# AdaLN scale and shift of the first 256 features: products summed on VectorE instead of row sums on TensorE

## The chip, the cores and the metric

The kernel runs on one core of one Trainium2 chip. The metric is the device time of one execution in microseconds (us); the engines are TensorE (PE, with PEld for its weight loads), VectorE (DVE), ScalarE (ACT), GpSimd (POOL) and SyncE (SP), which issues the transfers.

## The reference

A two-layer trunk over 512 tokens of 1024 features: stick-breaking attention and a gated token-mixing MLP, each followed by a SwiGLU layer. Every sub-layer has an RMSNorm in front whose result is scaled and shifted by numbers that depend on a conditioning vector `c`:

```python
def ada_modulation(c, w, b):
    m = jax.nn.silu(c) @ w + b
    shift, scale, gate = jnp.split(m, 3, axis=-1)
    return shift[:, None, :], scale[:, None, :], gate[:, None, :]
...
shift, scale, gate = ada_modulation(c, mix_ada_w[i], mix_ada_b[i])
h = rms_norm(x, mix_pre_g[i]) * (1.0 + scale) + shift
...
y = stick_breaking_mixer(h, sb_w_qkv[j], sb_w_o[j])
```

This case is about scale and shift of the very first sub-layer, so about the first 66 us of the kernel.

## The kernel before

All matrices are multiplied in float32 by splitting each operand into a high part (fp32r) and a remainder: ScalarE writes the high part (`wh`, `hTh`), VectorE subtracts it from the source to make the remainder (`wl`, `hTl`), and TensorE does three matmuls high x high, high x low, low x high (`mm3`). Line 94 records every matmul, line 102 every transpose, line 70 nearly every VectorE operation, line 161 and 162 the splits of a weight, line 117 other splits, line 111 every load on SyncE.

**The head.** Four tiles of 128 tokens (`x`) are loaded. `norm0` squares one on ScalarE, takes root and reciprocal, and scales it on VectorE; `turn0` transposes it on TensorE in two groups of four blocks (`tp`), and ScalarE or VectorE copies the blocks to `xhT`, which holds features on the partitions. From then on the 1024 features go in eight blocks of 128 (k = 0 to 7). For block k, `h0` has ScalarE multiply by the scale and add the shift (`xhT`, line 701), and splits the result to `hTh` and `hTl`. Then TensorE takes it as the contraction block k of the first half of the values (`v_step`: four token tiles, 12 matmuls `v`) and of the first head pair's queries and keys (`qk0_step`: 6 matmuls `pq` and `pk`). So each block brings 18 matmuls, and can start only when its scale and shift are there.

**Scale and shift.** They are products of `sc` (silu of c, 8 columns of 128) with a 1024x256 piece of weights per block, on their way for two blocks at a time. For blocks 2 to 7, three pairs, `ada0_sum` has POOL clear an accumulator (`acc`, 128x512) and VectorE add eight weight pieces, each times its column of `sc`; then `sums0` sums over the partitions with four small matmuls against a column of ones (into `ab`, which `cols0` has started with the bias), and VectorE multiplies by the norm's gain. Blocks 0 and 1 are done apart: `row0` has TensorE multiply the pieces (128x256) by the columns of `sc` directly, accumulates a row of 256 in `ab`, VectorE copies the row, and two small matmuls turn its halves into columns; `scales` adds the bias and multiplies by the gain.

**The gate.** Its weights (`rawada`) are added on VectorE in the same way into `G` (128x1024), in the background (`bg0.step`), from block 6 on.

A scheduler sets the order of the instructions of each engine from the order in which the code is written; an engine works strictly in its order. Buffers: `acc` has two (`acch`, `accl`), the `ada` pieces eight, `ab` takes turns in two PSUM banks.

## Time and profile before

| | |
|---|---|
| runs | 1131.42, 1133.75, 1135.18 us; median 1133.75 |
| profiled execution | 1135.34 us; its span 1133.6 us, mean granted clock 0.996 |
| busy | PE 1110.1, PEld 997.3, DVE 940.2, ACT 596.7, POOL 29.6 us |
| transfers | 176.39 MB in 51357 packets, mean 156 GB/s |
| chain that ended last | PE 78%, DMA 8%, DVE 8%, ACT 3%, issue 2% |

The span is from the first to the last recorded instruction. In a timeline row the first number is the start in us from the span's start, the second how long the merged instructions took, then engine, line, operation, output<-input, shapes and count; in brackets stands the idle time before it and what ended it. A group's row has after the bar the busy us and the mean ns of one.

### The profile page before, as it was taken

Reading aid. Unit: us, or ns where it says so; the run is one execution under the profiler, and the core shown is the slowest. Engines: PE = TensorE matmul, PEld = TensorE weight load, DVE = VectorE, ACT = ScalarE, POOL = GpSimd, SP = SyncE. Lnnn points to the kernel's source line nnn. Section 1 sums busy time; section 2 is a strip of 40 time slices with the busy share of each in tenths; the row PEclk is TensorE's granted clock in tenths of the full one; section 3 lists DMA queues with packets and bytes.
Section 4 is the critical chain, followed back from the end, with each engine's and each line's share of the span. In section 5 each row is a group of like instructions: output and inputs, shape, how many; then the busy total and the mean of one; then the engine's idle time right before and its main releaser. Section 6 shows DMA issues by size and latency. Waiting matters only on the chain.

```text
span 1133.6 us, 18637 instructions
## 1 busy us (share of the span) xinstructions
PE 1110.1 (98%) x7404; PEld 997.3 (88%) x7404; DVE 940.2 (83%) x1248; ACT 596.7 (53%) x982; POOL 29.6 (3%) x53
## 2 busy tenths in 40 slices
PE   6999999999999999999999999999999999999997
PEld 4787787788999999998878889988999999999996
DVE  4988999967989889778686967769979898889996
ACT  5454665656655555563143626437455555565752
POOL 0020100000000000010000000001000000000000
PEclk9999999999999999999999999999999999999999
DMA  7966434224434344438887375234243444223242
GB/s 301 353 219 213 147 104 131 76 72 150 149 121 140 127 154 130 131 115 307 268 276 241 131 241 177 83 131 158 86 131 114 165 131 141 71 87 98 91 164 95
DMA packets 51357, 176.39 MB, mean 156 GB/s; under 512 B 6075, under 2 KB 9147, under 8 KB 51269
## 3 DMA queue, kind: packets, MB, share of 16 engines
q1 hardware_dynamic: 48708, 166.81, 44.5%
q0 software_dynamic: 2560, 8.39, 2.1%
q8 instruction: 58, 0.95, 0.3%
q14 instruction: 31, 0.25, 0.1%
HBM read 164.69 MB, written 8.39 MB: 153 GB/s over the span
## 4 chain that ended last, share of the span: by engine, by line
PE 78%; DMA 8%; DVE 8%; ACT 3%; issue 2%; SPq 0%; POOL 0%; DVEq 0%; ACTq 0%
PE r L94 31%; PE y L94 9%; PE pqk L94 6%; PE v L94 5%; PE X L94 4%; PE u L94 4%; PE gu L94 4%; DMA rawada<-in_ada 4%; PE Y L94 3%; PE av L94 2%; PE z L94 2%; PE tw L102 1%; PE Z L94 1%; PE W L94 1%; PE tp L102 1%
## 5 line engine op out<-in xcount | busy, mean ns | idle before, releaser
L94 PE MATMUL r<-Sh,wl 128*128 128x256 f32 x608 | 169.9, 279 | 0.0
L94 PE MATMUL r<-Sh,wh 128*128 128x256 f32 x608 | 169.8, 279 | 0.0
L94 PE MATMUL r<-Sl,wh 128*128 128x256 f32 x608 | 169.7, 279 | 0.0
L161 ACT ACTIVATE wh<-raw 128x1024 fp32r<-128x1024 f32 x87 | 91.7, 1060 | 120.3 <-PE y L94 56.1
L94 PE MATMUL y<-wh,as 128*128 128x512 f32 x480 | 150.8, 391 | 0.4 <-DVE G L70 0.4
L117 ACT ACTIVATE wh<-f 128x1024 fp32r<-128x1024 f32 x87 | 92.4, 1062 | 90.0 <-PE r L94 66.6
L70 DVE TENSOR_TENSOR wl<-f,wh 128x1024 fp32r<-128x1024 f32 x87 | 106.4, 1223 | 39.0 <-ACT wh L117 38.9
L162 DVE TENSOR_TENSOR wl<-raw,wh 128x1024 fp32r<-128x1024 f32 x87 | 105.9, 1221 | 34.5 <-ACT wh L161 34.0
L94 PEld LDWEIGHTS r<-Sh,wl 128*128 128x128 f32 x608 | 114.1, 188 | 0.0
L94 PEld LDWEIGHTS r<-Sl,wh 128*128 128x128 f32 x608 | 114.1, 188 | 0.0
L94 PEld LDWEIGHTS r<-Sh,wh 128*128 128x128 f32 x608 | 113.9, 187 | 0.0
L94 PEld LDWEIGHTS y<-wh,as 128*128 128x128 f32 x480 | 90.0, 188 | 19.2 <-DVE G L70 0.8
L94 PE MATMUL y<-wl,as 128*128 128x512 f32 x240 | 93.7, 390 | 0.0
L94 PE MATMUL r<-hTh,wh 128*128 128x256 f32 x304 | 88.8, 293 | 0.5 <-DVE gu L70 0.4
L94 PE MATMUL r<-hTl,wh 128*128 128x256 f32 x304 | 84.8, 279 | 0.0
L94 PE MATMUL r<-hTh,wl 128*128 128x256 f32 x304 | 79.9, 279 | 0.0
L94 PEld LDWEIGHTS r<-hTh,wh 128*128 128x128 f32 x304 | 57.0, 187 | 5.8 <-DVE gu L70 2.1
L94 PE MATMUL r<-hTh,b 128*128 128x256 f32 x304 | 59.8, 279 | 0.0
L117 ACT ACTIVATE wh<-rawx 128x1024 fp32r<-128x1024 f32 x38 | 40.3, 1062 | 32.8 <-PE r L94 30.9
L94 PEld LDWEIGHTS r<-hTl,wh 128*128 128x128 f32 x304 | 57.1, 188 | 0.1
L94 PEld LDWEIGHTS r<-hTh,wl 128*128 128x128 f32 x304 | 55.0, 188 | 0.0
L94 PE MATMUL gu<-hTh,wh 128*128 128x256 f32 x192 | 53.8, 280 | 0.0
(272 smaller groups left out, 2955.0 us busy)
## 6 DMA issues: line engine op xcount, KB each, us to landing
rawada<-in_ada SPq DMA_DIRECT2D x80, 512.0 KB, 4.8
rawy<-in_wy SPq DMA_DIRECT2D x38, 512.0 KB, 3.5
rawx<-in_wx SPq DMA_DIRECT2D x38, 512.0 KB, 4.3
raw<-in_wdown SPq DMA_DIRECT2D x22, 512.0 KB, 4.5
raw<-in_wdn SPq DMA_DIRECT2D x22, 512.0 KB, 3.6
raw<-in_wqk SPq DMA_DIRECT2D x16, 512.0 KB, 4.6
ada<-in_ada0p SPq DMA_DIRECT2D x12, 512.0 KB, 7.9
raw<-in_wgu SPq DMA_DIRECT2D x12, 512.0 KB, 3.8
```

Of the source, the lines that this page charges most:

```text
L70: b = getattr(nc.vector, op)(*args, **kw)
L94: b = nc.tensor.matmul(o, l, r, start=start, stop=stop, skip_group_check=True)
L102: last_tp[0] = nc.tensor.transpose(o, i, ident)
L117: act.activation(hi, src, AF.Copy)
L161: act.activation(h[:], raw[:], AF.Copy)
L162: last_low[0] = nc.vector.tensor_tensor(l[:], raw[:], h[:].bitcast(F32), ALU.subtract)
```

## The change

`row0` is gone. In its place `pair0` uses `ada0_sum` on a width of 256: POOL clears 128x256 of an accumulator, VectorE adds eight pieces of 128x256, and two small matmuls sum over the partitions. `scales` is as before.

```diff
-    def row0(raws):
-
-        ps = bank("ab0", "p")
-        for q, raw in enumerate(raws):
-            for k in range(4):
-                mm(ps[0:1, :256], sc[:, q * 4 + k : q * 4 + k + 1], raw[:, k, :], q + k == 0, q * 4 + k == 7)
-        row = stp.tile([P, 256], F32, tag="row", bufs=2, name=nm("row"))
-        dve.tensor_copy(row[0:1, :], ps[0:1, :256])
+    def pair0(raws, tag):
+
+        acc = ada0_sum(raws, 256, 4, tag)
         ps = bank("ab0", "p")
         for i in range(2):
-            mm(ps[:, i : i + 1], row[0:1, i * P : (i + 1) * P], oneb[0:1, 0:1], True, True)
+            mm(ps[:, i : i + 1], acc[:, i * P : (i + 1) * P], onec, True, True)
         return ps
...
-    ab0 = row0(a0)
+    ab0 = pair0(a0, "acch")
...
-    ab1 = row0(a1)
+    ab1 = pair0(a1, "accl")
```

The places in the order on which the steps rest are two. On VectorE, before, between the scaling of the third x tile (`x_3`) and the remainder of the first scaled block (`hTl_133`); `ab` with `add` and `mul` is the scale and shift of block 0, `wl_251` the remainder of the first value weight:

```order
L70 TENSOR_SCALAR x_3_97<-x_3_97,r_183 128x1024
L70 COPY xhT_130<-tp_49_207 128x2x128
L70 COPY xhT_131<-tp_49_207 128x2x128
L70 RECIPROCAL r_219<-sd_217 128x1
L70 TENSOR_SCALAR x_4_99<-x_4_99,r_219 128x1024
L70 COPY row_195<-ab_45_186 1x256
L162 TENSOR_TENSOR wl_251<-raw_105,wh_250 128x1024
L70 TENSOR_TENSOR ab_262<-ab_47_197,add 128x2
L70 TENSOR_TENSOR ab_262<-ab_262,mul 128x2
```

And after, from the copies on to the first sum of block 1 (`acc_186` is the accumulator of block 0, `acc_267` that of block 1):

```order
L70 COPY xhT_130<-tp_48_206 128x2x128
L70 SCALAR_TENSOR_TENSOR acc_186<-ada_5_101,sc,acc_186 128x256
L70 COPY xhT_131<-tp_48_206 128x2x128
L70 SCALAR_TENSOR_TENSOR acc_186<-ada_5_101,sc,acc_186 128x256
L70 RECIPROCAL r_218<-sd_216 128x1
L70 SCALAR_TENSOR_TENSOR acc_186<-ada_5_101,sc,acc_186 128x256
L70 TENSOR_SCALAR x_4_99<-x_4_99,r_218 128x1024
L70 SCALAR_TENSOR_TENSOR acc_186<-ada_5_101,sc,acc_186 128x256
L70 SCALAR_TENSOR_TENSOR acc_186<-ada_6_103,sc,acc_186 128x256 x3
L162 TENSOR_TENSOR wl_250<-raw_105,wh_249 128x1024
L70 SCALAR_TENSOR_TENSOR acc_186<-ada_6_103,sc,acc_186 128x256
L70 SCALAR_TENSOR_TENSOR acc_267<-ada_8_107,sc,acc_267 128x256
```

The eight sums lie between the x tile's steps, and the weight's split stands ahead of the last of them.

On TensorE, before, from the transposes of the second x tile to the first value matmuls:

```order
L102 MATMUL tp_49_207<-identt,x_2_95 128x128 x4
L94 MATMUL ab_45_186<-ada_5_101,sc 1x256 x4
L94 MATMUL ab_45_186<-ada_6_103,sc 1x256 x4
L102 MATMUL tp_54_222<-identt,x_3_97 128x128 x4
L102 MATMUL tp_55_229<-identt,x_3_97 128x128
L94 MATMUL ab_47_197<-oneb,row_195 128x1 x2
L102 MATMUL tp_55_229<-identt,x_3_97 128x128 x3
L102 MATMUL tp_56_236<-identt,x_4_99 128x128 x4
L102 MATMUL tp_57_243<-identt,x_4_99 128x128 x4
L94 MATMUL ab_65_268<-ada_8_107,sc 1x256 x4
L94 MATMUL ab_65_268<-ada_9_109,sc 1x256 x4
L94 MATMUL v_70_286<-wh_250,hTh_132 128x512
```

And after, from the third x tile's transposes to the small matmuls of block 0:

```order
L102 MATMUL tp_53_221<-identt,x_3_97 128x128 x4
L102 MATMUL tp_54_228<-identt,x_3_97 128x128 x4
L102 MATMUL tp_55_235<-identt,x_4_99 128x128 x4
L102 MATMUL tp_56_242<-identt,x_4_99 128x128 x4
L94 MATMUL ab_46_196<-oneb,acc_186 128x1 x2
L94 MATMUL v_68_284<-wh_249,hTh_132 128x512
```

Nothing is left between the transposes, and the small matmuls of block 1 (`ab_65_277<-oneb,acc_267`) have moved from behind 8 value matmuls of block 0 to behind all 12 and two of `pq`.

Further down, VectorE has one sum of the next accumulator between the add and the multiply of block 1 in both programs, and SyncE has the first value weight of the second half ahead of five gate weights in both, the second one ahead of them in the changed order alone.

## The prediction

> **What bounds the kernel now.** I read the page first, then the busy time by stretch, then the timeline of the first 66 us, because the order of instructions differs there alone: on every engine the two programs list the same instructions in the same order again before the attention's second head pair.

> ```profile
> PE 1110.1 (98%) x7404; PEld 997.3 (88%) x7404; DVE 940.2 (83%) x1248; ACT 596.7 (53%) x982; POOL 29.6 (3%) x53
> 48.00:57.00 9.00, 9.00 (x44) 7.54 (x45) 8.76 (x13) 3.89 (x7) 0.00 (x0) 1.00 0.87 353
> 57.00:66.00 9.00, 9.00 (x42) 7.44 (x41) 8.86 (x9) 4.66 (x9) 5.03 (x11) 1.00 0.59 190
> 66.00:110.00 44.00, 43.83 (x213) 34.50 (x212) 35.52 (x39) 21.73 (x38) 4.16 (x8) 1.00 0.73 228
> 110.00:400.00 290.00, 287.40 (x1984) 253.61 (x1983) 252.65 (x324) 170.47 (x307) 7.22 (x12) 1.00 0.39 123
> ```

> After the stretch's bounds and its length stand the busy times of PE, PEld, DVE, ACT and POOL, then the granted clock, the DMA share and GB/s. From 48 us on TensorE has work all the time. So the question is when it reaches the steady part: what the head gains or loses there shifts the end by the same amount, since no later idle time takes it up. VectorE is nearly as full (8.76 of 9.00 and 8.86 of 9.00 us): this is where the change adds work.

> In the head TensorE stops in front of every new pair of features:

> ```profile
> 24.26 0.50 PE L94 MATMUL v<-wh,hTh 128*128 128x512 f32 x1
> 29.39 0.50 PE L94 MATMUL v<-wh,hTh 128*128 128x512 f32 x1 [0.33 <-ACT hTh L117]
> 36.65 0.80 PE L94 MATMUL v<-wh,hTh 128*128 128x512 f32 x1 [1.06 <-ACT hTh L117]
> 47.92 0.50 PE L94 MATMUL v<-wh,hTh 128*128 128x512 f32 x1 [0.40 <-ACT hTh L117]
> 57.15 0.39 PE L94 MATMUL v<-wh,hTh 128*128 128x512 f32 x1
> ```

> These are the starts of features 0, 1, 2, 4 and 6. I call them V0, V1, V2, V4 and V6; the change is worth what it moves V6.

> **What it removes.** Two times 16 pieces of row sum on TensorE, two copies of a row, and the small transposes of that row:

> ```profile
> 13.22 4.99 PE L94 MATMUL ab<-ada,sc 128*1 128x256 f32 x16
> 20.71 3.61 PE L94 MATMUL ab<-ada,sc 128*1 128x256 f32 x16
> 18.83 0.60 PE L94 MATMUL ab<-oneb,row 1*128 1x1 f32 x4
> L70 DVE COPY row<-ab 1x256 f32<-1x256 f32 x2 | 0.8, 408 | 3.3 <-PE ab L94 3.3
> ```

> The 8.6 us of row sums are on TensorE's path: the transposes of x's third and fourth tiles queue behind the first group, V0 behind the second. The small matmuls are replaced by as many over the full accumulator, which I take at the same 0.60 us.

> **What it adds.** Sixteen multiply-adds of 128x256 on VectorE. The trace has none of that width, but the same operation at 512 and at 1024:

> ```profile
> L70 DVE SCALAR_TENSOR_TENSOR acc<-ada,sc,acc 128x512 f32<-128x512 f32 x24 | 18.0, 750 | 0.6
> L70 DVE SCALAR_TENSOR_TENSOR G<-rawada,sc,G 128x1024 f32<-128x1024 f32 x3 | 3.8, 1282 | 0.0
> L70 DVE TENSOR_TENSOR hTl<-xhT,hTh 128x512 fp32r<-128x512 f32 x8 | 5.2, 686 | 3.1 <-ACT hTh L117 3.0
> L70 DVE COPY xhT<-tp 128x256 f32<-128x256 f32 x4 | 1.5, 418 | 0.3 <-PE tp L102 0.3
> 38.24 4.68 DVE L70 SCALAR_TENSOR_TENSOR acc<-ada,sc,acc 128x512 f32<-128x512 f32 x6
> ```

> 512 columns more cost 1282 - 750 = 532 ns, so 256 fewer cost 266 less: 484 ns. Six that depend on each other take 4.68 us, so one starts (4.68 - 0.75) / 5 = 0.79 us after the other, 0.04 more than its duration; I take 0.52 us in a chain and 0.40 where an independent instruction lies between. Bounds: 0.42 (a copy of that size) and 0.75 (the 512 form). Two groups of eight are about 8 us; less the two row copies, VectorE gets some 7 us more, in a stretch in which it has little idle time after 30 us.

> **The walk to V0.** The rows it hangs on:

> ```profile
> 13.32 0.76 DVE L70 COPY xhT<-tp 128x256 f32<-128x256 f32 x2 [0.30 <-PE tp L102]
> 14.19 0.75 DVE L70 TENSOR_SCALAR x<-x,r 128x1024 f32<-128x1024 f32 x1
> 18.58 1.20 DVE L162 TENSOR_TENSOR wl<-raw,wh 128x1024 fp32r<-128x1024 f32 x1
> 19.89 0.16 DVE L70 TENSOR_TENSOR ab<-ab,mul 128x2 f32<-128x2 f32 x1
> 21.55 0.85 ACT L701 ACTIVATE xhT<-xhT,ab 128x512 f32<-128x512 f32 x1
> 22.43 0.63 ACT L117 ACTIVATE hTh<-xhT 128x512 fp32r<-128x512 f32 x1
> ```

> Now the scale is ready at 20.05 but ScalarE, behind the late transposes, takes it up at 21.55; hTh is ready at 23.1, and TensorE is still in the second row sum until 24.25. In the changed order VectorE starts summing at 13.66. With the two copies, the reciprocal and the x tile between them, seven sums end near 18.0; the wl split comes ahead of the eighth (18.0 to 19.2), the eighth ends at 19.6. The x tile comes about 1.1 us later than now, which its transposes (done by 18) and ScalarE (done by 18.6) absorb. Two small matmuls to 20.25, add, one sum of the next group, multiply at 20.75 to 20.9; scale and split as now: V0 at 22.5, 1.75 us earlier. This is all the change gains.

> **From V0 to V1.** Between 18 and 22.5 TensorE now has only the small matmuls. What a gap does to its clock:

> ```profile
> 26.26:29.68 3.42, 3.09 (x17) 2.65 (x17) 2.67 (x6) 1.79 (x3) 0.00 (x0) 1.00 0.90 315
> 33.09:36.50 3.41, 2.50 (x16) 2.12 (x15) 3.24 (x5) 1.94 (x3) 1.42 (x2) 1.00 0.50 156
> 36.50:39.92 3.42, 3.27 (x8) 2.62 (x9) 3.35 (x6) 1.68 (x3) 0.00 (x0) 0.50 0.92 334
> 37.24 0.63 PE L94 MATMUL v<-wl,hTh 128*128 128x512 f32 x1
> 37.67 0.63 PE L94 MATMUL v<-wh,hTh 128*128 128x512 f32 x1
> 57.60 0.39 PE L94 MATMUL v<-wh,hTh 128*128 128x512 f32 x1
> 57.83 0.39 PE L94 MATMUL v<-wl,hTh 128*128 128x512 f32 x1
> ```

> After a stretch with 2.50 of 3.41 us busy the clock was 0.50 for 3.4 us, and matmuls started 0.43 us apart instead of 0.23; after one with 3.09 busy it stayed at 1.00. So V0's matmuls start at half clock, on the profile's own grid until 26.26: nine at 0.43, then five at 0.23, and the fourteen that stand ahead of the second small group end at 27.5 (bounds 25.7 at full clock throughout, 28.5 at half). VectorE has ended the second group at 25.4, with the hTl and wl splits in between, so TensorE, not VectorE, is last here.

> ```profile
> 26.30 0.60 PE L94 MATMUL ab<-oneb,row 1*128 1x1 f32 x4
> 26.93 0.16 DVE L70 TENSOR_TENSOR ab<-ab,add 128x2 f32<-128x2 f32 x1 [0.69 <-PE ab L94]
> 27.67 0.15 DVE L70 TENSOR_TENSOR ab<-ab,mul 128x2 f32<-128x2 f32 x1
> 34.36 0.16 DVE L70 TENSOR_TENSOR ab<-ab,mul 128x4 f32<-128x4 f32 x1
> 45.63 0.16 DVE L70 TENSOR_TENSOR ab<-ab,mul 128x4 f32<-128x4 f32 x1 [1.57 <-PE ab L94]
> 33.38 0.95 PE L94 MATMUL ab<-oneb,acc 128*128 128x1 f32 x8
> ```

> Now the multiply follows the small matmuls' start (26.30) by 1.37 us, with a sum between add and multiply, and V1 the multiply by 1.72. The same from 27.5: multiply at 28.9, V1 at 30.6, 1.2 us later than now. TensorE idles about 1.7 us before it.

> **From V1 to V6.** From that multiply VectorE needs 7 sums of 0.78, one hTl and one wl split, 6.3 us, until the next accumulator is whole: 35.3. TensorE has 20 matmuls ahead of its small group: six at half clock until 33.1 and fourteen at 0.23, to 36.3 (at full clock 35.1, and VectorE is last). Small matmuls 0.95, and from the multiply 2.29 to the matmuls (34.36 to 36.65 now): V2 at 39.6, 3.0 later than now. The idle time before it is over 2 us, so the half clock that costs 1.4 us there now (seven matmuls at 0.20 more) costs as much again. 27 matmuls and the small group take VectorE's multiply to 48.5 against 45.63, V4 to 50.8 (+2.9). The next accumulator is whole at about 56.4 and TensorE ready for it at 56.3; V6 at 60.1 against 57.15: **+3.0 us**.

> The other effects I take at zero, with their covers.

> ```profile
> rawada<-in_ada SPq DMA_DIRECT2D x8, 512.0 KB, 9.0
> ```

> The accumulators' clearings on POOL now wait for the small matmuls, and end at 21, 29 and 38 us, ahead of their sums at 25.4, 36.5 and 46. SyncE's queue has the second-half value weight ahead of five gate weights, held until a wl split near 55.7; the gate sums that need them stand behind two splits, near 64, and now they land 9.0 us after their issue. If they come later, VectorE stalls on them while TensorE still has 24 matmuls, 5.4 us, per value weight.

> [...] The trace has the half clock after an idle time of 1.06 us. [...]

> **The sum.** The profiled execution took 1135.34 us, 1.74 over its span of 1133.6; plus 3.0 is 1138.3. The median of the three runs is 1.59 lower, so on it 1133.75 + 3.0 = **1136.8 us** (+0.27%), just under the 0.3% (3.4 us) that a measurement of this kernel can tell from no change.

> **Rivals.**
> - *Half clock throughout* (25%, with dearer sums). All fourteen matmuls after V0 run at 0.43, and eight after V1 as well: V1 at 31.6, V2 at 41.0, V4 at 52.1, V6 at 61.5: +4.4, 1138.2. Sums of 0.75 instead of 0.48 move the second group to 29.7 and come to some +5. For it: the gaps before V0, V1 and V2 are all longer than the 1.06 us that sufficed; against it: full clock came back after one stretch. It decides if more than eleven of the fourteen run at half clock.
> - *Short gaps cost no clock* (12%). Then V1 stands at 30.6 but V2 is bound by VectorE, 38.9, and the matmuls after it run at full clock: its multiply at 46.5 waits for VectorE's sums alone (+0.8), V6 at 58.2: +1.05, 1134.8. The 0.50 row speaks against it. [...]
> - *Not slower* (6%). TensorE is at full clock from V0 on: the small group ends by 26.3, V1 at 28.9, V2 at 36.75 without a drop, V6 at 56.3: -0.9, 1132.9. It needs the small matmuls to keep the clock up; no row shows that.
> - *The change does nothing*: excluded, since the listing shows the sums on VectorE.

> **Chances and range.** My walk has 55%. The runs scatter by 1.4 us above their median and 2.3 below, so its +3.0 falls on either side of 3.4: 0.25 slower, 0.30 same. The first rival adds 0.24 to slower and 0.01 to same, the second 0.12 to same, the third 0.03 each to faster and same; 0.02 are left, half faster, half slower. That makes faster 0.04, same 0.46, slower 0.50. The range goes from 0.8 us below the second rival, 1134.0, to 1.4 us above the first, 1139.6.

> **What would show it.** Right: V0 near 22.5 with matmuls 0.43 apart, V1 after an idle time of over 1.5 us, V2 near 39.6 with the clock at 0.50, V6 near 60, and equal distances from there. Wrong: 256-wide sums off 0.48 us; full clock after V0; a V2 before 38; or a stall on a gate weight after 60 us.

## The result and the profile after

The changed kernel takes 1139.74 us in the median of seven runs (1137.31 to 1142.75), the kernel before, run beside it seven times, 1131.42 us (1128.80 to 1135.18): ratio 1.0068, 95% interval 1.0048 to 1.0089. That is slower, by some 7.7 us; forecast were 3.0 us, and the range ended 0.14 us below the measured median. The profiled execution took 1141.10 us, its span is 1139.2.

The page of the changed kernel, busy time of the engines:

```profile
span 1139.2 us, 18594 instructions
PE 1106.9 (97%) x7372; PEld 999.5 (88%) x7372; DVE 946.0 (83%) x1262; ACT 595.3 (52%) x982; POOL 30.2 (3%) x55
```

VectorE has 5.8 us more, TensorE 3.2 us less, although TensorE ran part of its matmuls at half clock. So the longer time is not more work: TensorE is idle for longer, and part of its busy time is at half clock. TensorE's timeline, with the small matmuls of block 0 and then the starts V0, V1, V2, V4 and V6:

```profile
18.62 1.01 PE L94 MATMUL ab<-oneb,acc 128*128 128x1 f32 x4 [2.32 <-DVE acc L70]
21.92 0.80 PE L94 MATMUL v<-wh,hTh 128*128 128x512 f32 x1 [2.29 <-ACT hTh L117]
30.70 0.80 PE L94 MATMUL v<-wh,hTh 128*128 128x512 f32 x1 [1.81 <-ACT hTh L117]
40.25 0.50 PE L94 MATMUL v<-wh,hTh 128*128 128x512 f32 x1 [1.69 <-ACT hTh L117]
51.40 0.50 PE L94 MATMUL v<-wh,hTh 128*128 128x512 f32 x1 [0.17 <-ACT hTh L117]
60.63 0.39 PE L94 MATMUL v<-wh,hTh 128*128 128x512 f32 x1
```

V0 comes 2.34 us earlier than in the profile before, V1 already 1.31 later, V6 3.48 later. In front of V0, V1 and V2 stand idle times of 1.7 to 2.3 us, where the kernel before had none, 0.33 and 1.06. What they do to the clock is in the busy time by stretch (the clock is the first number after the five busy times), cut where the clock changed:

```profile
13.60:17.00 3.40, 1.39 (x11) 0.94 (x9) 3.29 (x9) 3.39 (x10) 0.00 (x0) 1.00 1.03 422
17.00:20.41 3.41, 1.01 (x4) 0.93 (x4) 2.70 (x8) 0.42 (x3) 0.53 (x1) 0.51 1.02 416
20.41:23.82 3.41, 1.90 (x5) 1.51 (x6) 3.30 (x7) 2.38 (x3) 0.00 (x0) 0.50 0.63 258
23.82:27.24 3.42, 3.42 (x10) 2.65 (x9) 1.68 (x3) 0.00 (x0) 0.00 (x0) 0.50 0.49 128
27.24:30.66 3.42, 1.65 (x12) 1.48 (x10) 2.36 (x5) 1.45 (x3) 0.53 (x1) 0.99 1.02 416
30.66:34.07 3.41, 3.37 (x8) 2.72 (x9) 3.32 (x5) 1.89 (x2) 0.00 (x0) 0.50 0.55 226
34.07:37.48 3.41, 3.41 (x19) 2.86 (x18) 2.48 (x3) 0.00 (x0) 0.00 (x0) 0.99 0.45 136
37.48:40.90 3.42, 1.73 (x10) 1.32 (x11) 2.87 (x6) 2.75 (x5) 1.42 (x2) 1.00 1.00 384
40.90:44.31 3.41, 3.41 (x10) 2.63 (x9) 3.30 (x6) 0.76 (x1) 0.00 (x0) 0.50 1.03 418
```

Each stretch here in which TensorE was busy for only 1.0 to 1.9 of its 3.4 us is followed by one at 0.50; after each full one (3.37 to 3.42) the clock is back. At 0.50 the value matmuls start 0.43 us apart, at 0.99 they start 0.23 us apart. So the gaps that the chain of sum, small matmul, multiply, scale and split leaves in TensorE can cost twice: once as idle time, and once in the matmuls behind them. Which of the two makes the loss, the fillers below tell.

A second loss stands where the prediction did not look. The sum of the gate's rows (`av<-accl`), before, and then after:

```profile
98.11 0.50 PE L94 MATMUL av<-accl,ones 128*128 128x512 f32 x1 [0.17 <-DVE accl L70]
```

```profile
102.93 0.50 PE L94 MATMUL av<-accl,ones 128*128 128x512 f32 x1 [1.51 <-DVE accl L70]
```

From V6 up to this matmul the two programs keep a distance of 3.5 us, behind it 4.8. The chain that ended last in the changed kernel leads from there back to a transfer (start, duration, what):

```profile
90.15 1.12 DVE wl L157
91.28 0.02 issue
91.29 5.86 DMA raw<-in_wqk
97.15 0.02 issue
97.17 1.07 ACT wh L156
...
102.28 0.61 DVE accl L70
...
102.93 0.50 PE av L94
```

A piece of the query and key weights, issued only when the split before it has released its buffer, arrives at 97.15; ScalarE and VectorE split it, and on VectorE a scan and the gate sum stand behind that split.

Ahead of this the order differs from that of the kernel before. On ScalarE the first high part of these weights (`wh`, line 156) stood ahead of the four `ga` that wait for TensorE's z, and now stands behind two of them, before and then after:

```profile
76.72 1.06 ACT L156 ACTIVATE wh<-raw 128x1024 fp32r<-128x1024 f32 x1 [2.20 <-DMA raw<-in_wqk]
78.21 1.19 ACT L890 ACTIVATE ga<-z 128x128 f32<-128x128 f32 x4
```

```profile
80.98 0.66 ACT L885 ACTIVATE ga<-z 128x128 f32<-128x128 f32 x2 [2.73 <-PE z L94]
81.52 1.06 ACT L156 ACTIVATE wh<-raw 128x1024 fp32r<-128x1024 f32 x1
```

### The profile page after: what moved, and what is told of

It is laid out like the page before. It is cut to its first block, busy times and chain, and to the rows that moved or that the text cites. A ratio compares the mean times of both kernels' runs of the same rounds, so it can differ in the third digit from the quotient of the medians.

```text
span 1139.2 us, 18594 instructions
## 1 busy us (share of the span) xinstructions
PE 1106.9 (97%) x7372; PEld 999.5 (88%) x7372; DVE 946.0 (83%) x1262; ACT 595.3 (52%) x982; POOL 30.2 (3%) x55
## 3 DMA queue, kind: packets, MB, share of 16 engines
q1 hardware_dynamic: 48708, 166.81, 44.2%
## 4 chain that ended last, share of the span: by engine, by line
PE 88%; DVE 5%; ACT 2%; DMA 2%; issue 2%; SPq 0%; DVEq 0%; ACTq 0%
PE r L94 32%; PE y L94 17%; PE v L94 7%; PE pqk L94 6%; PE X L94 4%; PE u L94 4%; PE gu L94 4%; PE Y L94 3%; PE av L94 2%; PE z L94 2%; PE tw L102 1%; PE Z L94 1%; PE W L94 1%; PE tp L102 1%; DVE f L70 1%
## 5 line engine op out<-in xcount | busy, mean ns | idle before, releaser
L94 PE MATMUL r<-Sh,wl 128*128 128x256 f32 x608 | 169.8, 279 | 0.0
L94 PE MATMUL r<-Sh,wh 128*128 128x256 f32 x608 | 169.8, 279 | 0.0
L94 PE MATMUL r<-Sl,wh 128*128 128x256 f32 x608 | 169.6, 279 | 0.0
L94 PE MATMUL y<-wh,as 128*128 128x512 f32 x480 | 150.7, 391 | 0.0
L117 ACT ACTIVATE wh<-f 128x1024 fp32r<-128x1024 f32 x87 | 92.3, 1061 | 89.8 <-PE r L94 66.8
L70 DVE TENSOR_TENSOR wl<-f,wh 128x1024 fp32r<-128x1024 f32 x87 | 106.3, 1222 | 38.9 <-ACT wh L117 38.8
L162 DVE TENSOR_TENSOR wl<-raw,wh 128x1024 fp32r<-128x1024 f32 x87 | 105.7, 1220 | 35.7 <-ACT wh L161 35.3
L94 PEld LDWEIGHTS r<-Sh,wl 128*128 128x128 f32 x608 | 114.1, 188 | 0.0
L94 PEld LDWEIGHTS r<-Sl,wh 128*128 128x128 f32 x608 | 114.0, 188 | 0.0
L94 PEld LDWEIGHTS r<-Sh,wh 128*128 128x128 f32 x608 | 114.0, 187 | 0.0
L94 PEld LDWEIGHTS y<-wh,as 128*128 128x128 f32 x480 | 90.0, 188 | 19.0 <-DVE G L70 0.4
L94 PE MATMUL y<-wl,as 128*128 128x512 f32 x240 | 93.6, 390 | 0.0
L94 PE MATMUL r<-hTh,wh 128*128 128x256 f32 x304 | 88.8, 292 | 0.7 <-DVE gu L70 0.7
L94 PE MATMUL r<-hTl,wh 128*128 128x256 f32 x304 | 84.8, 279 | 0.0
L94 PE MATMUL r<-hTh,wl 128*128 128x256 f32 x304 | 80.0, 279 | 0.0
L94 PEld LDWEIGHTS r<-hTh,wh 128*128 128x128 f32 x304 | 57.0, 187 | 6.0 <-DVE gu L70 2.4
L94 PE MATMUL r<-hTh,b 128*128 128x256 f32 x304 | 59.8, 279 | 0.0
L94 PE MATMUL v<-wh,hTh 128*128 128x512 f32 x128 | 53.2, 415 | 6.0 <-ACT hTh L117 6.0
L117 ACT ACTIVATE wh<-rawx 128x1024 fp32r<-128x1024 f32 x38 | 40.3, 1061 | 32.5 <-PE r L94 30.9
L94 PEld LDWEIGHTS r<-hTl,wh 128*128 128x128 f32 x304 | 57.1, 188 | 0.1
L94 PEld LDWEIGHTS r<-hTh,wl 128*128 128x128 f32 x304 | 55.0, 188 | 0.0
## 6 DMA issues: line engine op xcount, KB each, us to landing
rawada<-in_ada SPq DMA_DIRECT2D x80, 512.0 KB, 4.6
rawy<-in_wy SPq DMA_DIRECT2D x38, 512.0 KB, 3.6
rawx<-in_wx SPq DMA_DIRECT2D x38, 512.0 KB, 3.9
raw<-in_wdown SPq DMA_DIRECT2D x22, 512.0 KB, 4.3
raw<-in_wdn SPq DMA_DIRECT2D x22, 512.0 KB, 3.6
raw<-in_wqk SPq DMA_DIRECT2D x16, 512.0 KB, 5.8
ada<-in_ada0p SPq DMA_DIRECT2D x12, 512.0 KB, 5.9
raw<-in_wgu SPq DMA_DIRECT2D x12, 512.0 KB, 4.0
```

Source lines behind the costliest of these rows:

```text
L70: b = getattr(nc.vector, op)(*args, **kw)
L94: b = nc.tensor.matmul(o, l, r, start=start, stop=stop, skip_group_check=True)
L117: act.activation(hi, src, AF.Copy)
L162: last_low[0] = nc.vector.tensor_tensor(l[:], raw[:], h[:].bitcast(F32), ALU.subtract)
```

## The experiments

Theories: **T1**, TensorE loses at half clock behind its new gaps; **T2**, VectorE's sums themselves are the loss; **T3**, the order past 70 us, which the change shifted without meaning to, costs at the gate sum.

**The changed kernel with filler matmuls in the gaps.** 31 matmuls that nobody reads; VectorE, ScalarE and SyncE as in the changed kernel.

```diff
+    warm(8)
     ab0 = pair0_turn(ab0)
+    warm(8)
...
+            warm(8, last_pq[0])
             v_step(vb, 0, 1, wv0[0])
...
+                warm(7, pe["prev"])
             v_step(vb, 0, 2 * b - 2, wv0[b - 1])
```

> The changed kernel with 31 extra matmuls of 128x512 on TensorE whose results nobody reads: 8 in front of and 8 behind the small matmuls of block 0, 8 in the gap before feature 1, 7 in the gap before feature 2. Every other engine has the same instructions in the same order as the changed kernel. Theory half clock (the gaps cost the clock, and the clock costs the time): granted clock 1.00 through the head, V1 near 29 (30.7 in the changed kernel), V2 near 37.2 (40.3), V6 near 56.5 (60.6), and the total some 3 to 4.4 us below the changed kernel, a ratio to before of about 1.003, because the wait for the gate sums near 100 us stays. Theory VectorE load (the eight added sums per block bind the head whatever TensorE's clock): V2 stays at 39 or later, V6 at 59.5 or later, ratio 1.006 or more.

Measured: 1134.06 us, ratio 1.0017 (1.0006 to 1.0029). Its timeline, fillers, V0 and the gate sum:

```profile
19.37 2.09 PE L94 MATMUL warm<-wh 128*128 128x512 f32 x8
21.80 0.50 PE L94 MATMUL v<-wh,hTh 128*128 128x512 f32 x1 [0.34 <-ACT hTh L117]
97.16 0.50 PE L94 MATMUL av<-accl,ones 128*128 128x512 f32 x1 [1.22 <-DVE accl L70]
```

The granted clock is 1.00 in all stretches of the head, and the multiply of features 6 and 7 starts at 52.49 instead of 57.96; V6 is 5.5 us earlier. From V0, V1 and V2 to the small matmuls that follow each, the changed kernel takes 2.5, 1.5 and 1.6 us longer than this one. That is all of it: the difference lies in the matmuls behind the gaps, while the gaps are no shorter than before, only filled. Against the changed kernel the fillers take 0.0051 of the time, 5.8 us: T1 has most of the loss. VectorE's sums are all still there, so T2 cannot have it. The wait of 1.22 us on the gate sum stays.

**The kernel before with four fillers ahead of feature 2.**

```diff
         if b > 1:
+            if b == 2:
+                warm(4, pe["prev"])
             v_step(vb, 0, 2 * b - 2, wv0[b - 1])
```

> The kernel before with 4 extra matmuls nobody reads in the one long gap of its head, before feature 2; nothing else moves. Theory half clock: V2 stays at 36.7, the matmuls behind it run 0.23 us apart instead of 0.43, V4 and V6 come about 1.2 us earlier (VectorE's idle time of 1.57 us before the multiply at 45.6 allows no more), ratio to before 0.999. [...]

Measured: 1132.18 us, ratio 1.0000 (0.9987 to 1.0013). The fillers gain nothing that can be seen; the interval is too wide to shut out the expected 0.999. **A second profile of the kernel before**, unchanged, asks directly whether the half clock behind V2 is usual:

> The kernel before, unchanged, for a second profile of it. If its usual execution has no half clock ahead of feature 2, as the filler experiment on it suggests: V2 (the first value matmul of feature 2) near 35.3 to 36.7 with matmuls 0.23 us apart behind it, the multiply of features 4 and 5 near 44.2 instead of 45.63, the span near 1131.5 to 1132.5. If the drop is usual: a stretch at 0.50 behind V2 again and a span near 1133.6. Time ratio 1.000 either way.

The profiled execution took 1132.12 us (median of ten runs 1132.46, ratio 1.0007, 0.9995 to 1.0019). V0, V2 and V4, and the stretches around V2:

```profile
22.89 0.50 PE L94 MATMUL v<-wh,hTh 128*128 128x512 f32 x1
35.29 0.50 PE L94 MATMUL v<-wh,hTh 128*128 128x512 f32 x1 [1.07 <-ACT hTh L117]
45.09 0.50 PE L94 MATMUL v<-wh,hTh 128*128 128x512 f32 x1 [0.40 <-ACT hTh L117]
```

```profile
34.10:37.51 3.41, 2.34 (x13) 1.84 (x12) 3.38 (x6) 2.55 (x4) 0.34 (x1) 1.00 0.94 328
37.51:40.92 3.41, 3.41 (x17) 2.82 (x16) 3.23 (x6) 0.17 (x1) 0.00 (x0) 1.00 1.02 417
```

The same gap (1.07 us against 1.06), and no drop. Against the first profile V2 is 1.36 us earlier, V4 2.83: 1.47 is the missing half clock. The rest lies ahead of V0. The second x tile's transposes start 0.43 us earlier, since that tile landed earlier. And the first group of row sums is 0.9 us shorter: its matmuls start 0.43 us apart, as at half clock, until 13.6 us here and until 16.1 us in the first profile, and 0.22 us apart from there on (the group takes 4.04 us here and 4.99 there). So the first profile was an unfavourable one in three ways.

How often a drop falls into the kernel before can be estimated from the mean clock of its 85 executions beside the experiments, since one stretch of 3.41 us at 0.50 takes 0.0015 off it. 26 have 0.996 or 0.997, as the first profile has (0.996), and take 1134.0 us in the median; 59 have 0.998 or 0.999, as the second has (0.998), and take 1131.4 us. Read this way, about one execution in three has a drop, and the median has none.

**One block alone.** Block 0 on VectorE and block 1 with row sums; and the reverse (edits against the changed kernel, with `row0` back in it).

```diff
-    ab1 = pair0(a1, "accl")
+    ab1 = row0(a1)
```

> Block 0 summed on VectorE as in the changed kernel, block 1 with row sums on TensorE as before. SyncE's order and VectorE's order after the head are those of before. Theory of the walk: the row sums of block 1 now lie in the gap before V0 and delay it (V0 24 to 25.5) but later there is no added VectorE work: V1 near 29.8, V2 near 37.2, no wait for gate sums near 100 us, total 0.5 to 1 us over before, ratio 1.0005 to 1.001. Rival (each block's sums on VectorE cost half of the change): ratio 1.003 to 1.004.

Measured: 1135.23 us, ratio 1.0028 (1.0018 to 1.0039).

```diff
-    ab0 = pair0(a0, "acch")
+    ab0 = row0(a0)
```

> Block 0 with row sums on TensorE as before, block 1 summed on VectorE as in the changed kernel; SyncE's order and VectorE's order after the head are those of the changed kernel. Theory of the walk: V0 near 23.1, matmuls partly at half clock, V1 30 to 31, V2 39 to 40, V6 2.5 to 3.5 later than before, and the wait for gate sums near 100 us of 1.3 us on top: ratio 1.004 to 1.006. Rival (half of the change each): ratio 1.003 to 1.004.

Measured: 1136.98 us, ratio 1.0046 (1.0030 to 1.0063). One stretch of half clock of each, the first with block 0 on VectorE, then with block 1:

```profile
18.10:24.90 6.80, 5.28 (x15) 2.26 (x16) 3.70 (x6) 2.68 (x5) 0.53 (x1) 0.50 0.73 299
```

```profile
21.10:28.00 6.90, 6.15 (x15) 4.81 (x16) 3.77 (x6) 1.61 (x3) 0.00 (x0) 0.51 0.56 202
```

The first ratio is above what the walk had expected and just under the rival's range, the second is where the walk had it. In either profile the block on VectorE opens a gap of 2.3 us, and half clock follows it. With block 0 alone the row sums of block 1 fall into it (5.74 us instead of 3.61), and V0 comes only at 26.23. The gate sum waits 0.69 us in the first, whose order past the head is that of the kernel before, and 1.45 us in the second, whose order is the changed one: a first sign for T3.

**The VectorE sums without the gap.** The kernel before with the sixteen sums added into accumulators that nobody reads; the row sums stay.

```diff
+    ada0_sum(a0, 256, 4, "acch")
...
+    ada0_sum(a1, 256, 4, "accl")
```

> The kernel before with the sixteen VectorE sums of the changed kernel added, into accumulators that nothing reads; the row sums on TensorE stay, so TensorE has no new gap before V0, and VectorE has the 8 us of extra sums. If the loss is TensorE's half clock behind its gaps: V0 within 1 us of 24.3, no half clock before feature 2, and the time 0 to +3 us over the kernel before (some from sums that stand ahead of a multiply, some from the late order). If the loss is VectorE's 8 us of sums, in a stretch in which it has little idle time: V6 at least 4 us later than in the kernel before, and the time +4 to +8 us.

Measured: 1141.88 us, ratio 1.0083 (1.0058 to 1.0107): slower than the change, and more than either theory allowed. The multiply of features 6 and 7 is at 54.44, 3.0 us later than in the second profile of before, and V6 is 3.4 us later, not 4. The rest comes at the gate sum, and then from the clock behind it:

```profile
103.04 0.79 PE L94 MATMUL av<-accl,ones 128*128 128x512 f32 x1 [2.66 <-DVE accl L70]
```

```profile
98.71:102.12 3.41, 1.10 (x4) 0.37 (x2) 3.41 (x3) 2.20 (x5) 0.00 (x0) 1.00 0.81 247
102.12:105.53 3.41, 2.49 (x6) 2.01 (x7) 3.41 (x6) 0.46 (x1) 0.00 (x0) 0.50 0.22 50
105.53:108.94 3.41, 3.41 (x10) 2.63 (x9) 2.27 (x2) 0.00 (x0) 0.00 (x0) 0.50 0.69 235
```

Instruction by instruction the distance is 3.4 us at V6 (waits on `acc` and `hTh`, and one stretch at half clock), 7.8 at this matmul, 10.6 when the clock is back. So this run does not separate T1 from T2, since the added work also shifted the order past 70 us; but it shows T3's wait in a larger size, and that a late wait loses clock as an early one does.

**The order past 70 us moved back.** The changed kernel, without and with the fillers. Not every row stands again where it stood before: the first high part `wh` of the query and key weights is ahead of the two `ga` that wait for z, and three remainders `wl` are earlier among the steps of vs, A and U.

```diff
+                            if i == 0 and js == B31:
+                                order(last_act[0], qk_high[0])
...
+            if len(u_steps) > 1:
+                order(b, qk_low[(0, 1, 2)[len(u_steps) - 2]])
```

> The changed kernel; past 70 us the first high part of the query and key weights stands ahead on ScalarE of the two activations ga that wait for z, behind which the change had moved it, and three remainders of those weights stand ahead on VectorE of steps of vs, A and U. TensorE's and SyncE's lists are those of the changed kernel. If the idle time of 1.51 us ahead of the second av matmul comes from this order, through weights that land later: that idle time falls to 0.2 to 0.7 us and the time is 1.0 to 2.0 us below the changed kernel's 1139.7 (ratio to the kernel before 1.005 to 1.006). If it comes from the head being late, or from transfers whatever the order: the idle time stays at 1.2 us or more and the time is within 0.5 us of 1139.7.

Measured: 1137.36 us, ratio 1.0055 (1.0033 to 1.0077). The transfer in its chain, and the gate sum:

```profile
89.09 4.53 DMA raw<-in_wqk
```

```profile
99.40 0.50 PE L94 MATMUL av<-accl,ones 128*128 128x512 f32 x1 [0.48 <-DVE accl L70]
```

The wait falls from 1.51 to 0.48 us. The transfer starts 2.2 us earlier than in the changed kernel, but this says nothing of the order: the head of this execution had two stretches fewer at half clock, and its multiply of features 6 and 7 stands at 55.50 instead of 57.96. Counted from that multiply the transfer starts 0.3 us later; it takes 4.53 us instead of 5.86, and lands 1.1 us earlier. The gate sum gains the same 1.1 us.

> The changed kernel with both: the 31 filler matmuls in TensorE's gaps, whose output nothing reads, and the late order. If half clock and late order are all of the loss: no half clock, the idle time ahead of the second av matmul below 0.7 us, and the time 0.5 us over to 1.5 us under the kernel before (ratio 0.9985 to 1.0005). If the late idle time does not come from the order: as with the fillers alone, ratio near 1.0017.

Measured: 1132.16 us, ratio 0.9997 (0.9986 to 1.0009); the clock is 1.00 in the head, and the gate sum does not wait. The transfer again starts no earlier than with the fillers alone (86.28 against 85.82), and takes 3.47 us instead of 5.56. In both pairs of traces the transfer is shorter with the order moved back; why was not measured. The four together:

| ratio to the kernel before | order as changed | order moved back |
|---|---|---|
| gaps open | 1.0068 | 1.0055 |
| gaps filled | 1.0017 | 0.9997 |

The fillers take 0.0051 and 0.0058 (5.8 and 6.6 us), the order 0.0013 and 0.0020 (1.5 and 2.3 us), and with both nothing is left of the loss. The order's part without fillers lies inside the two intervals; its wait in the trace carries that reading. With the fillers the intervals just overlap.

**Work in place of fillers.** Block 0 on VectorE, block 1 with row sums, half of them ahead of block 0's small matmuls, half behind.

```diff
+    row0_half(rowps, a1[0], 0)
+    ab0 = pair0_turn(ab0)
+    row0_half(rowps, a1[1], 1)
```

> Block 0 is summed on VectorE as in the changed kernel, block 1 by row sums on TensorE as before; but half of those row sums stand ahead of block 0's small matmuls and half behind them, where TensorE waited. Past the head the order is that of the kernel before. If a late start of TensorE costs only through its clock: no half clock before V0, V0 at 21.3 to 22.0 against 22.9 in the usual execution of before, V1 near 26.5 to 27.2 (before 28.0), no wait of more than 0.7 us on the gate sum; the time 0 to 1.5 us under the kernel before if no drop falls ahead of feature 2 (ratio 0.9987 to 1.0000), up to 1.4 us over it where one does. If sums on VectorE themselves cost the head time: V1 and V2 no earlier than in the kernel before, and the time 1 to 3 us over it.

Measured: 1131.99 us, ratio 0.9994 (0.9980 to 1.0007). Its timeline, row sums, V0 and V2, and the stretch behind V2:

```profile
19.51 1.89 PE L94 MATMUL ab<-ada,sc 128*1 128x256 f32 x8
21.59 0.50 PE L94 MATMUL v<-wh,hTh 128*128 128x512 f32 x1 [0.20 <-ACT hTh L117]
34.36 0.62 PE L94 MATMUL v<-wh,hTh 128*128 128x512 f32 x1 [0.93 <-ACT hTh L117]
```

```profile
34.42:37.83 3.41, 3.41 (x9) 2.63 (x10) 3.34 (x6) 1.17 (x2) 0.00 (x0) 0.53 1.01 395
```

These are the second eight row sums. V0 is 1.3 us and V1 (26.29) 1.7 us ahead of the second profile of before, V2 0.9; then this execution had the drop behind V2.

> As the one before, with four filler matmuls more (read by nobody) in the gap ahead of feature 2, against a drop there. If that gap is the last that can cost clock: no half clock in the profile, the time 0 to 1.5 us under the kernel before (ratio 0.9987 to 1.0000), and never above the version without the fillers by more than 0.3 us. If V2 is bound by VectorE's sums: the gain of V0 and V1 is lost in a longer gap ahead of V2 and the ratio is 1.000.

Measured: 1131.91 us, ratio 0.9998 (0.9983 to 1.0013), no half clock. V2 is at 35.68, no earlier than before: in this execution V0 (22.75) was early by 0.14 us only, with the first eight row sums spread over 3.18 us instead of 1.89: they start 0.39 us apart in the mean instead of 0.22, near the 0.43 of half clock. Neither version beats the kernel before by more than the measurement can tell; no version tried does.

## Why the prediction was right and wrong

Right: slower, through TensorE's clock behind its new gaps, and not through TensorE's or VectorE's busy time; though its own chances, 0.50 for slower and 0.46 for same, left open whether a measurement would see it. The sum on VectorE had been taken at 484 ns and 0.52 us in a chain; it is 0.48, and four take 2.04:

```profile
12.70 0.48 DVE L70 SCALAR_TENSOR_TENSOR acc<-ada,sc,acc 128x256 f32<-128x256 f32 x1
15.00 2.04 DVE L70 SCALAR_TENSOR_TENSOR acc<-ada,sc,acc 128x256 f32<-128x256 f32 x4
```

Wrong was the size: 3.0 us against some 7.7. Three steps failed. That V1, V2 and V6 still stand within 0.7 us of the times forecast for them (30.6, 39.6 and 60.1) is luck: the second x tile landed 0.97 us earlier than in the profile before, which hid a longer half clock.

- **"From V0 to V1", half clock until 26.26.** It lasted until 27.24, so that twelve of the fourteen matmuls ran at half clock, and V1's and V2's followed in turn. That is the first rival, *half clock throughout*, by its own condition (more than eleven). How much earlier the x tile landed, its transposes show, before and after:

```profile
11.32 1.97 PE L102 MATMUL tp<-identt,x 128*128 128x128 f32 x8 [1.98 <-DVE x L70]
```

```profile
10.35 3.57 PE L102 MATMUL tp<-identt,x 128*128 128x128 f32 x16 [1.02 <-DVE x L70]
```

  Add these 0.97 us, and V1, V2, V4 and V6 stand at 31.67, 41.22, 52.37 and 61.60, where the rival had 31.6, 41.0, 52.1 and 61.5: +4.4 us instead of +3.0. The changes of the clock in the profile before (36.50 and 39.92 us) were carried over in steps of 3.41 us to another execution, where the clock changed at other times (17.04, 27.28 and 30.69 us).
- **"the half clock that costs 1.4 us there now ... costs as much again".** The step took this half clock as common to both kernels. The kernel before has it in about one execution of three, and the second profile has none, so 1.47 us more belong to the change; and 0.9 us of the first profile's row sums are its late start of the full clock. V6 is 6.3 us behind the second profile of before (54.34 to 60.63), 3.5 behind the first. The median of three runs on which the sum was made, 1133.75, came out 2.3 us lower with seven.
- **"The other effects I take at zero", and "the order of instructions differs there alone", in the first 66 us.** The cover named, at 64 us, held. But between 70 and 90 us the order on ScalarE, VectorE and SyncE differed, and behind it a transfer of weights landed late for the gate sum near 100 us: 1.4 us from V6's distance to the one behind the gate sum (6.29 to 7.73 against the second profile), 1.5 to 2.3 us by the runs. Moving ScalarE's and VectorE's order back, with SyncE's as changed, took away 1.0 of the 1.5 us of that wait, and with the fillers all of it.

Added up, 4.4, 1.5, 0.9 and 1.4 us make 8.2, against the 7.7 measured over all runs.

After the stretch from 27.24 to 30.66, in which TensorE was busy for 1.65 us and never idle for longer than 1.81, the clock was 0.50. In the traces of both kernels the recorded changes of the clock lie whole multiples of 3.41 us apart, but at different times: the first record begins at 16.02 us in the kernel before, and the clock changes 20.48 and 23.89 us behind it; it begins at 13.63 us in the changed kernel, and the clock changes 3.41, 13.65 and 17.07 us behind it. Of two executions of the kernel before, with a gap of 1.06 and of 1.07 us at the same place, one lost its clock and one did not.

Of the remaining rivals, *short gaps cost no clock* fell with the first stretch at 0.50. *Not slower* needed full clock from V0 on; with fillers to provide it and the order moved back the head comes out even (V0 21.37, V2 35.96 and V4 45.49, against 22.89, 35.29 and 45.09 in the second profile), so its gain of 0.9 us is not there either: the multiply ahead of V2 hangs on VectorE's sums and splits, and takes back what V0 gained.

## What to carry to other kernels

TensorE work that looks removable may be what keeps the clock up: without the row sums TensorE had gaps of 1.7 to 2.3 us in front of V0, V1 and V2, and with fillers in them the clock stayed at 1.00 and the kernel took 5.8 us less. Before work is moved off TensorE, count what stands in its place, and price a gap by the matmuls behind it that run at half speed (here 2.5, 1.5 and 1.6 us behind V0, V1 and V2), not by its length. An effect of one execution, such as a clock drop (1.47 us here), is no part of a baseline until a second profile shows it. A change early in the program is compared in order up to the point where the lists agree for good; a swapped instruction can cost where a later transfer lands: here the order between 70 and 90 us cost 1.5 to 2.3 us by the runs, at a gate sum near 100 us.

## What was not expected of the hardware

Ahead of the first record the profile counts a clock of 1.00, but TensorE ran at the pace of half clock there: the first row sums of the kernel before start 0.43 us apart until 16.1 us and 0.22 us apart from there on, with the first record at 16.0; the changed kernel's transposes start 0.21 us apart until 13.6 us and 0.11 us apart from 15.2 us on, with the first record at 13.6. So the mean clock of an execution leaves out its start. This limits the account above: that half clock makes the loss of the head is read from the profiled executions, while the other executions have only a mean clock, and with block 0 alone three of twelve have 0.998 or 0.999 and are no faster (1133.84 to 1136.77 us). Whether these had their half clock at the start, or lost the time in another way, the record does not show.
